# A streaming encoder step: where the attention's reciprocal and the split of a head pair's outputs stand in their turns

## The chip, the cores and the metric

The kernel runs as one program on one core of a Trainium2 chip. The metric is the device time of one execution in microseconds (us). The kernel before has been timed three times: 2195.16, 2206.37 and 2203.8 us, with a median of 2203.8 us. A further execution, which was profiled, took 2202.2 us, and all rows below come from that one.

## The reference, cut to what matters

One trunk layer of a chunk-causal encoder handles 1024 prompt frames and 64 sample frames (1088 columns in all, model width 1024, 16 heads of 64). The part that matters here is the attention beside the input projection:

```
h = rms_norm(x, norm_mix)
glu_a, glu_b, q, k, v, gates = split(h @ w_in)
u = glu_a * sigmoid(glu_b);  c = causal_dwconv(u, width 31);  c = silu(layer_norm(c)) @ w_conv_out
sc = q @ k.T * dh**-0.5 + rel_bias          # each 64-frame chunk sees itself and the 8 chunks before
pr = softmax(sc, axis=-1)
a  = (pr @ v) @ w_att_out
x  = x + (sigmoid(gates_c) * c + sigmoid(gates_a) * a) @ w_out
```

A gated feed-forward block, an input embedding and a last norm follow. All of it is float32. The products with weights are made of three products each, since every float32 operand is split into a rounded high part and a remainder.

## The kernel before, in words

Activations lie feature by row, time by column. The first stage works through a list of units, each a 1024 x 128 slice of `w_in` of one kind: `gb` and `ga` (the two halves of the gated unit), `s` (branch gates), and `q`, `k`, `v` for one pair of heads. A unit is computed in three column groups (384, 384 and 320 columns). `mm3` makes the 24 matmuls of a group, and calls a hook once in the middle of them. `job_group` makes the group, lets the helper engines read its result out of PSUM (`evac`), and calls the same hook once more. So there are six calls a unit, one for every 12 projection matmuls. Between two units `w_ahead` splits the next weights (`w_split`, L134 on ScalarE and L135 on VectorE).

The hook is `tick`, and one call of it is a *turn*. Attention is threaded through the projections by it. A step of attention is one head and one block of 128 queries (the ninth block is the 64 sample queries). Each head pair has 18 steps, and each is carried over several turns:

- `step_S`: TensorE makes the scores into `s_ps`, and VectorE adds the bias and takes the row extreme in one instruction (L487), which also frees `s_ps`. The pool that holds `s_ps` has one buffer.
- `step_E`, at the end of the same turn: ScalarE takes the exponential and the row sums (L495).
- `step_R`, one turn later: VectorE takes the reciprocal of the sums (L517) and ScalarE scales the row by it (L518).
- `step_T`, two turns after the scores: TensorE transposes the probabilities into `t_ps` (L504) and ScalarE copies them to `pt` (L507). `t_ps` has one buffer as well.
- `step_PV`, in every second turn, once both heads of a pair have their `pt`: TensorE multiplies by the values into `o_ps` (L529, 20 matmuls at full length). `o_ps` also has one buffer.
- `step_AT`, before the change at the end of the turn after `step_PV`: `split_into` copies `o_ps` to the high part of `aT` on ScalarE (L170), subtracts on VectorE to get the remainder (L171), and GpSimd's queue stores `aT` (L537). L171 is the last reader of `o_ps`.

Each engine runs its instructions in the order in which the program issues them, and that order is written out by hand (`manual_schedule`): it is the order of the calls inside `tick` and of the code around it. Inside a turn `bg_tick` also issues pieces of the depthwise convolution (taps, L327, on VectorE) and, once all eight features are convolved, of the layer norm (on both helper engines). How many it issues follows from a budget counted in estimated TensorE time, not from what the engines do. A turn with `step_PV` is called an A turn below, the one after it a B turn. A turns come at the end of a column group, B turns in the middle of one.

Of the kernel before, what the change touches and what calls it, by code (L numbers as in the profile page):

```python
# [75 lines left out]
def encoder_step(ctx: ExitStack, tc: tile.TileContext, I, O):  # L76
    nc = tc.nc
# [90 lines left out]
    def split_into(dst, c0, n, src, scale=1.0):  # L168

        nc.scalar.activation(out=dst[:, 0, c0:c0 + n], in_=src, func=AF.Copy, scale=scale)  # L170
        nc.vector.scalar_tensor_tensor(out=dst[:, 1, c0:c0 + n], in0=src, scalar=scale,  # L171
                                       in1=dst[:, 0, c0:c0 + n].bitcast(F32), op0=ALU.mult, op1=ALU.subtract)
# [47 lines left out]
    with tc.manual_schedule():  # L220
# [53 lines left out]
        at = att.enter_context(tc.tile_pool(name="att", bufs=1))  # L274
# [29 lines left out]
        bg = []  # L304
        debt = [0.0]

        def bg_tick(budget, most):
            debt[0] = min(debt[0] + budget, 2.5)
            while bg and debt[0] > 0 and most > 0:
                cost, fn = bg.pop(0)  # L310
                fn()
                debt[0] -= cost
                most -= 1
# [144 lines left out]
        for h in range(2):  # L458
            nc.gpsimd.memset(ql[h][64 - 64 * h:128 - 64 * h, :].bitcast(F32), 0.0)
        pipe = []  # L460
        stages = {"e": [], "t": [], "pv": [], "at": []}

        def step_S(st):
            i, p, h = st["i"], st["p"], st["h"]
            c = cur[i]
            smp = p == 8
            m = SMP if smp else P
            q0 = P * p
            if smp:
                n, k0, b0 = PAST + SMP, SEQ, 0  # L470
            else:
                k0 = max(0, P * p - PAST)
                n = P * p + P - k0
                b0 = 640 - n
            st.update(m=m, n=n, vb=(8 if smp else k0 // P), q0=q0)
            nh, w = (2, n // 2) if n > 512 else (1, n)
            ps = ps_s.tile([P, 2, 512], F32, tag="s", name="s_ps")
            wm = max(w, 256)
            for x in range(nh):
                a = k0 + x * w  # L480
                nc.tensor.matmul(ps[0:m, x, 0:wm], lhsT=c["Q"][h][:, q0:q0 + m], rhs=c["K"][h][:, a:a + wm],
                                 start=True, stop=False)
                nc.tensor.matmul(ps[0:m, x, 0:wm], lhsT=ql[h][:, q0:q0 + m], rhs=c["K"][h][:, a:a + wm],  # L483
                                 start=False, stop=True)
            s = at.tile([P, 640], F32, tag="s", name="s", bufs=3)
            sm = at.tile([P, 3], F32, tag="sm", name="sm", bufs=6)
            nc.vector.tensor_tensor_reduce(  # L487
                out=s[0:m, 0:n].rearrange("p (x c) -> p x c", x=nh), in0=ps[0:m, 0:nh, 0:w],
                in1=c["bias"][h][0:m, b0:b0 + n].rearrange("p (x c) -> p x c", x=nh),
                scale=1.0, scalar=3e38, op0=ALU.add, op1=ALU.min, accum_out=sm[0:m, 0:1])  # L490
            st.update(s=s, sm=sm)

        def step_E(st):
            m, n, s, sm = st["m"], st["n"], st["s"], st["sm"]
            nc.scalar.activation(out=s[0:m, 0:n], in_=s[0:m, 0:n], func=AF.Exp, scale=-1.0, bias=sm[0:m, 0:1],  # L495
                                 accum_out=sm[0:m, 1:2])

        def step_T(st):
            m, n, s = st["m"], st["n"], st["s"]
            nb = (n + P - 1) // P  # L500
            ps = ps_t.tile([P, 1024], F32, tag="t", name="t_ps")
            for b in range(nb):
                w = min(P, n - b * P)
                nc.tensor.transpose(ps[0:w, b * P:b * P + m], s[0:m, b * P:b * P + w], ident[0:m, 0:m])  # L504
            pt = at.tile([P, 640], F32, tag="pt", name="pt", bufs=2)
            if m == P:
                nc.scalar.activation(out=pt[:, 0:n], in_=ps[:, 0:n], func=AF.Copy)  # L507
            else:
                nc.scalar.activation(out=pt[:, 0:512].rearrange("p (b q) -> p b q", q=P)[:, :, 0:m],
                                     in_=ps[:, 0:512].rearrange("p (b q) -> p b q", q=P)[:, :, 0:m], func=AF.Copy)  # L510
                nc.scalar.activation(out=pt[0:64, 512:512 + m], in_=ps[0:64, 512:512 + m], func=AF.Copy)
            st.update(pt=pt, nb=nb)

        def step_R(st):

            m, n, s, sm = st["m"], st["n"], st["s"], st["sm"]
            nc.vector.reciprocal(out=sm[0:m, 2:3], in_=sm[0:m, 1:2])  # L517
            nc.scalar.activation(out=s[0:m, 0:n], in_=s[0:m, 0:n], func=AF.Copy, scale=sm[0:m, 2:3])  # L518

        def step_PV(pair):  # L520

            st = pair[0]
            c, m, n, nb = cur[st["i"]], st["m"], st["n"], st["nb"]
            o_ps = ps_o.tile([P, 512], F32, tag="o", name="o_ps")
            for b in range(nb):
                w = min(P, n - b * P)
                for x in pair:
                    a = 64 * x["h"]
                    nc.tensor.matmul(o_ps[a:a + 64, 0:m], lhsT=c["v"][0:w, st["vb"] + b, a:a + 64],  # L529
                                     rhs=x["pt"][0:w, b * P:b * P + m], start=(b == 0), stop=(b == nb - 1))  # L530
            st["o"] = o_ps

        def step_AT(st):
            m = st["m"]
            aT = at.tile([P, 2, P], F32R, tag="aT", name="aT")
            split_into(aT, 0, m, st["o"][:, 0:m])
            dma_st(out=a_d[st["i"]][:, :, st["q0"]:st["q0"] + m], in_=aT[:, :, 0:m].bitcast(F32))  # L537

        pe_bg = []

        def tick(base=1.95):


            spent = base
            pair = len(stages["pv"]) == 2
            late = len(stages["t"]) > 1 or (stages["t"] and not pipe)
            if pair:
                spent += 0.218 * stages["pv"][0]["nb"] + 0.2
            if late:
                spent += 0.107 * ((stages["t"][0]["n"] + P - 1) // P)  # L550
            if pipe:
                spent += 0.5
            ready_at = bool(stages["at"])
            new = pipe.pop(0) if pipe else None
            if new is not None:
                step_S(new)
            for x in stages["e"]:
                step_R(x)
            stages["e"].clear()
            bg_tick(RATIO * spent, 1)  # L560
            if pair:
                step_PV(stages["pv"])
                stages["at"].append(stages["pv"][0])
                stages["pv"].clear()
            if late:
                st = stages["t"].pop(0)
                step_T(st)
                stages["pv"].append(st)
            if new is not None:
                step_E(new)  # L570
                stages["e"].append(new)
                stages["t"].append(new)
            if ready_at:
                step_AT(stages["at"].pop(0))
            if pe_bg:
                if pe_bg[0][0] <= 0:
                    pe_bg.pop(0)[1]()
                else:
                    pe_bg[0][0] -= 1
            bg_tick(0.0, 9)  # L580
# [55 lines left out]
        def job(kind, i):  # L636
            hl = job_begin(kind, i)
            for g in range(3):
                job_group(kind, i, g, hl)
                if g == 0:  # L640
                    w_ahead(1)

        def job_group(kind, i, g, hl):
            c0, n = GR[g]
            ps_full = pjp.tile([P, 512], F32, tag="pj", name="pj")
            mm3(ps_full[:, 0:n], hl, hT, c0, n, hook=tick)
            evac(kind, i, g, ps_full[:, 0:n])
            tick()
# [236 lines left out]
        xt = None  # L885
        for kind, i in order_1a[2:-1]:
            job(kind, i)
        while pipe or stages["t"] or stages["pv"] or stages["at"] or pe_bg or bg:
            tick()
        att.close()  # L890

# [67 lines left out]
        for f in range(KT):  # L959
# [14 lines left out]
            x = xc.tile([P, T], F32, tag="xc", name="x")  # L974
# [691 lines left out]
```

## Time and profile before

| | |
|---|---|
| median of three runs | 2203.8 us |
| profiled execution, its own time | 2202.2 us |
| its span, first to last instruction | 2200.0 us |
| busy share of the span | PE 95%, PEld 93%, DVE 62%, ACT 40%, POOL 10% |
| mean granted TensorE clock | 0.985 of full speed |
| stage with attention | from about 100 us to about 1005 us |

PE is TensorE's matmuls, PEld its weight loads, DVE is VectorE, ACT ScalarE, POOL GpSimd. A row of the trace names a line of the program, an engine, an operation, what it writes and from what. In brackets stands how long the engine sat idle ahead of it and which instruction ended that wait. The granted clock is told as a share of full speed: 1.00 is 2.4 GHz and 0.50 is 1.2 GHz. In a list of waits a line gives who waited, on whom, the total in us, how many times, and the longest.

### The profile page before, as it was taken

What the parts mean: (1) busy time and instruction counts of PE and PEld (TensorE: products, weight loads), DVE (VectorE), ACT (ScalarE), POOL (GpSimd) and SP (SyncE); (2) the same over time, 40 slices, a digit from 0 to 9 for tenths busy, and PEclk for the clock granted to TensorE, in tenths of its full rate; (3) what the DMA queues carried; (4) which work ended last, traced back from release to release, by engine and by line L of the source; (5) the groups of instructions that cost most, each with busy time, mean ns of one, the idle gap of its engine ahead of it and who ended that gap; (6) DMA issues with size and microseconds to landing.
All of it is one profiled execution on the core that took longest, in us unless ns stands there. A gap on an engine that the chain in (4) does not pass through costs nothing.

```text
span 2200.0 us, 35326 instructions
## 1 busy us (share of the span) xinstructions
PE 2100.2 (95%) x14472; PEld 2039.9 (93%) x14472; DVE 1359.4 (62%) x2310; ACT 872.3 (40%) x1695; POOL 230.7 (10%) x455
## 2 busy tenths in 40 slices
PE   8989999999999998979999999999999999999997
PEld 6979898888888898879999999999999999999997
DVE  6777777777777663444235467777777763345644
ACT  5453635455555445574012334333333332112421
POOL 5100101101010101111000000000000020000400
PEclk9999999999999999999999999999999999999999
DMA  3312121212121221113433331212212144331011
GB/s 137 104 35 90 64 77 57 92 49 89 50 86 50 92 73 58 69 49 140 185 135 130 116 130 59 89 62 86 89 59 89 70 159 168 123 121 45 10 58 54
DMA packets 64706, 192.53 MB, mean 88 GB/s; under 512 B 8368, under 2 KB 22976, under 8 KB 63200
## 3 DMA queue, kind: packets, MB, share of 16 engines
q1 hardware_dynamic: 43072, 104.00, 13.9%
q0 software_dynamic: 21328, 85.71, 10.9%
q8 instruction: 114, 1.87, 0.3%
q10 hardware_dynamic: 144, 0.56, 0.1%
q14 instruction: 48, 0.39, 0.1%
HBM read 146.18 MB, written 54.01 MB: 91 GB/s over the span
## 4 chain that ended last, share of the span: by engine, by line
PE 50%; DVE 3%; issue 3%; ACT 2%; DMA 0%; POOL 0%; POOLq 0%; DVEq 0%; ACTq 0%
PE pj L1175 7%; PE pj L1176 7%; PE pj L1174 7%; PE pj L159 7%; PE pj L160 6%; PE pj L161 6%; PE pj L1477 3%; PE pj L1476 3%; PE pj L1475 3%; DVE acc L1021 1%; PE o_ps L529 0%; ACT tmp L1020 0%; ACT s L495 0%; ACT c L407 0%; PE t_ps L504 0%
## 5 line engine op out<-in xcount | busy, mean ns | idle before, releaser
L159 PE MATMUL pj<-hT,whl 128*128 128x384 f32 (+1 forms) x1296 | 445.6, 344 | 5.6 <-ACT kst L708 2.4
L161 PE MATMUL pj<-hT,whl 128*128 128x384 f32 (+1 forms) x1296 | 427.9, 330 | 0.3 <-DVE whl L135 0.3
L160 PE MATMUL pj<-hT,whl 128*128 128x384 f32 (+1 forms) x1296 | 427.7, 330 | 0.0
L327 DVE SCALAR_TENSOR_TENSOR c<-u,cc,c 128x1118 f32<-128x1118 f32 x240 | 329.7, 1374 | 3.4
L159 PEld LDWEIGHTS pj<-hT,whl 128*128 128x128 f32 x1296 | 247.4, 191 | 11.4 <-ACT kst L708 4.0
L160 PEld LDWEIGHTS pj<-hT,whl 128*128 128x128 f32 x1296 | 247.5, 191 | 0.0
L161 PEld LDWEIGHTS pj<-hT,whl 128*128 128x128 f32 x1296 | 246.7, 190 | 0.6 <-DVE whl L135 0.6
L1174 PE MATMUL pj<-mp,wq 128*128 128x272 f32 x704 | 203.9, 290 | 3.8 <-ACT ug L1250 2.7
L1176 PE MATMUL pj<-mp,wq 128*128 128x272 f32 x704 | 204.2, 290 | 0.0
L1175 PE MATMUL pj<-mp,wq 128*128 128x272 f32 x704 | 204.0, 290 | 0.0
L134 ACT ACTIVATE whl<-raw 128x1024 fp32r<-128x1024 f32 (+3 forms) x100 | 100.1, 1001 | 221.9 <-PE pj L1477 134.2
L518 ACT ACTIVATE s<-s,sm 128x640 f32<-128x640 f32 (+3 forms) x144 | 101.7, 706 | 194.2 <-DVE sm L517 192.7
L135 DVE TENSOR_TENSOR whl<-raw,whl 128x1024 fp32r<-128x1024 f32 (+3 forms) x100 | 115.7, 1158 | 91.9 <-ACT whl L134 91.8
L487 DVE CUSTOM_DVE_ANT_0 s<-s_ps,bias 128x640 f32<-128x640 f32 (+3 forms) x144 | 95.6, 664 | 110.9 <-PE s_ps L483 94.1
L1151 ACT ACTIVATE wq<-raw 128x512 fp32r<-128x512 f32 x144 | 84.3, 625 | 189.9 <-DVE raw L1160 135.6
L1476 PE MATMUL pj<-gp,whl 128*128 128x384 f32 (+1 forms) x432 | 141.2, 327 | 0.3 <-DVE gp L1385 0.3
L1477 PE MATMUL pj<-gp,whl 128*128 128x384 f32 (+1 forms) x432 | 141.2, 327 | 0.2 <-DVE whl L135 0.2
L1475 PE MATMUL pj<-gp,whl 128*128 128x384 f32 (+1 forms) x432 | 140.9, 326 | 0.0
L1175 PE MATMUL pj<-bq,wq 128*128 128x272 f32 x480 | 138.6, 289 | 0.0
L1176 PE MATMUL pj<-bq,wq 128*128 128x272 f32 x480 | 138.3, 288 | 0.0
L1174 PE MATMUL pj<-bq,wq 128*128 128x272 f32 x480 | 138.2, 288 | 0.0
L1174 PEld LDWEIGHTS pj<-mp,wq 128*128 128x128 f32 x704 | 133.8, 190 | 4.3 <-ACT ug L1250 2.9
(258 smaller groups left out, 4844.5 us busy)
## 6 DMA issues: line engine op xcount, KB each, us to landing
raw<-in_w_in SPq DMA_DIRECT2D x56, 512.0 KB, 3.2
raw<-in_w_ffn_up SPq DMA_DIRECT2D x44, 512.0 KB, 4.2
q_d<-ug POOLq DMA_DIRECT2D x22, 544.0 KB, 3.0
gp<-q_d POOLq DMA_DIRECT2D x22, 544.0 KB, 7.1
tg<-s_d POOLq DMA_DIRECT2D x16, 544.0 KB, 3.9
aP<-a_d POOLq DMA_DIRECT2D x8, 1088.0 KB, 6.0
a_d<-aT POOLq DMA_DIRECT2D x64, 128.0 KB, 2.2
f_d<-e_d POOLq DMA_DIRECT2D x16, 383.5 KB, 5.0
```

What stands on the lines that cost most here:

```text
L135: nc.vector.tensor_tensor(out=hl[:, 1, 0:k, :], in0=raw[:, 0:k, :], in1=hl[:, 0, 0:k, :].bitcast(F32), op=ALU.subtract)
L159: nc.tensor.matmul(ps, lhsT=wsel(hl, 0, k), rhs=r[:, 0, c0:c0 + n], start=(k == 0), stop=False)
L160: nc.tensor.matmul(ps, lhsT=wsel(hl, 0, k), rhs=r[:, 1, c0:c0 + n], start=False, stop=False)
L161: nc.tensor.matmul(ps, lhsT=wsel(hl, 1, k), rhs=r[:, 0, c0:c0 + n], start=False, stop=(k == K - 1))
L327: nc.vector.scalar_tensor_tensor(out=c_t[f], in0=u_t[f][:, j:j + CCOL], scalar=pc("conv_dw", f * CW + j), in1=c_t[f], op0=ALU.mult, op1=AL ...
L518: nc.scalar.activation(out=s[0:m, 0:n], in_=s[0:m, 0:n], func=AF.Copy, scale=sm[0:m, 2:3])
L1174: nc.tensor.matmul(ps, lhsT=q[:, 0, kt, :], rhs=h, start=start and kt == 0, stop=False)
L1175: nc.tensor.matmul(ps, lhsT=q[:, 0, kt, :], rhs=l, start=False, stop=False)
L1176: nc.tensor.matmul(ps, lhsT=q[:, 1, kt, :], rhs=h, start=False, stop=stop and kt == 3)
L1475: nc.tensor.matmul(ps, lhsT=hl[:, 0, k, :], rhs=h, start=k == 0, stop=False)
L1476: nc.tensor.matmul(ps, lhsT=hl[:, 0, k, :], rhs=l, start=False, stop=False)
L1477: nc.tensor.matmul(ps, lhsT=hl[:, 1, k, :], rhs=h, start=False, stop=k == K - 1)
```

## The change

VectorE's reciprocals of the waiting steps move out of `step_R` to the head of the turn, ahead of `step_S`. The line that scales the row stays where it was. `step_AT` moves from the end of the next turn to the place right behind `step_PV`, so the list of pairs that waited for it goes.

```diff
-        stages = {"e": [], "t": [], "pv": [], "at": []}
+        stages = {"e": [], "t": [], "pv": []}
...
         def step_R(st):
 
             m, n, s, sm = st["m"], st["n"], st["s"], st["sm"]
-            nc.vector.reciprocal(out=sm[0:m, 2:3], in_=sm[0:m, 1:2])
             nc.scalar.activation(out=s[0:m, 0:n], in_=s[0:m, 0:n], func=AF.Copy, scale=sm[0:m, 2:3])
...
-            ready_at = bool(stages["at"])
+            for x in stages["e"]:
+                nc.vector.reciprocal(out=x["sm"][0:x["m"], 2:3], in_=x["sm"][0:x["m"], 1:2])
             new = pipe.pop(0) if pipe else None
             if new is not None:
                 step_S(new)
...
             bg_tick(RATIO * spent, 1)
             if pair:
                 step_PV(stages["pv"])
-                stages["at"].append(stages["pv"][0])
+                step_AT(stages["pv"][0])
                 stages["pv"].clear()
             if late:
                 st = stages["t"].pop(0)
                 step_T(st)
...
-            if ready_at:
-                step_AT(stages["at"].pop(0))
...
-        while pipe or stages["t"] or stages["pv"] or stages["at"] or pe_bg or bg:
+        while pipe or stages["t"] or stages["pv"] or pe_bg or bg:
```

Two lines fewer in front of it move the line numbers behind the change: L517 for the reciprocal becomes L553, L518 for the scaling becomes L517; the evacuation of `u`, L666 before, is L664 after.

The places shown are an A turn of the third head pair and the B turn behind it, with a weight split between them. In the trace of before this is the stretch from 381.4 to 392.1 us. First VectorE's queue before; L487 is the read of the scores (its second row the row extreme), L327 a tap, L135 the remainder of the split weights:

```order
L487 ISA s,sm<-s_ps,bias 128x640
L487 ISA sm 128x1
L517 RECIPROCAL sm<-sm 128x1
L327 SCALAR_TENSOR_TENSOR c<-u,cc,c 128x1118 x2
L135 TENSOR_TENSOR whl<-raw,whl 128x1024
L487 ISA s,sm<-s_ps,bias 128x640
L487 ISA sm 128x1
L517 RECIPROCAL sm<-sm 128x1
L327 SCALAR_TENSOR_TENSOR c<-u,cc,c 128x1118
L171 SCALAR_TENSOR_TENSOR aT<-o_ps,aT 128x128
```

And VectorE's queue in the same two turns after the change:

```order
L553 RECIPROCAL sm<-sm 128x1
L487 ISA s,sm<-s_ps,bias 128x640
L487 ISA sm 128x1
L327 SCALAR_TENSOR_TENSOR c<-u,cc,c 128x1118
L171 SCALAR_TENSOR_TENSOR aT<-o_ps,aT 128x128
L327 SCALAR_TENSOR_TENSOR c<-u,cc,c 128x1118
L135 TENSOR_TENSOR whl<-raw,whl 128x1024
L553 RECIPROCAL sm<-sm 128x1
L487 ISA s,sm<-s_ps,bias 128x640
L487 ISA sm 128x1
L327 SCALAR_TENSOR_TENSOR c<-u,cc,c 128x1118
```

The reciprocal now stands ahead of the read of the new scores, and the remainder L171 stands in the A turn, between two taps, where it stood at the end of the B turn.

ScalarE's queue in the same two turns, before; L518 scales, L507 copies `pt`, L495 is the exponential, L134 the high part of the weights, L170 the high part of the outputs:

```order
L518 ACTIVATE s<-s,sm 128x640
L507 ACTIVATE pt<-t_ps 128x640
L495 ACTIVATE s,sm<-s,sm 128x640
L134 ACTIVATE whl<-raw 128x1024
L518 ACTIVATE s<-s,sm 128x640
L507 ACTIVATE pt<-t_ps 128x640
L495 ACTIVATE s,sm<-s,sm 128x640
L170 ACTIVATE aT<-o_ps 128x128
```

And after, where L517 is the scaling:

```order
L517 ACTIVATE s<-s,sm 128x640
L170 ACTIVATE aT<-o_ps 128x128
L507 ACTIVATE pt<-t_ps 128x640
L495 ACTIVATE s,sm<-s,sm 128x640
L134 ACTIVATE whl<-raw 128x1024
L517 ACTIVATE s<-s,sm 128x640
L507 ACTIVATE pt<-t_ps 128x640
L495 ACTIVATE s,sm<-s,sm 128x640
```

The copy L170 moved from the end of the B turn to the second place of the A turn, ahead of the copy of `pt` and the exponential. Which instructions there are, and TensorE's order, stay as they were.

## Rows read from the trace of the kernel before

**Rows 1.** The list of waits of TensorE over the whole span: who waited, for whom, us in total, times, longest.

```profile
PE o_ps L529 <- DVE aT L171: 51.8, 49, 3.4
PE o_ps L529 <- DVE sm L517: 6.3, 5, 1.3
PE s_ps L481 <- DVE sm L487: 2.7, 3, 1.6
```

**Rows 2.** Busy time by stretch: the stage with attention, and one pair of turns from the start of the scores of one A turn to the next. Columns: the stretch and its length, then busy us and instructions of PE, PEld, DVE, ACT and POOL, the granted clock, the DMA share and GB/s.

```profile
60.00:1012.00 952.00, 877.96 (x6050) 831.45 (x6049) 626.80 (x999) 497.84 (x1079) 106.64 (x204) 0.98 0.21 70
381.36:389.80 8.44, 7.94 (x63) 7.46 (x63) 6.88 (x12) 4.57 (x9) 0.67 (x1) 1.00 0.10 26
```

**Rows 3.** Groups of instructions by line over the whole span: busy us, mean ns of one, then the engine's idle time just ahead of them and what ended it.

```profile
L518 ACT ACTIVATE s<-s,sm 128x640 f32<-128x640 f32 (+3 forms) x144 | 101.7, 706 | 194.2 <-DVE sm L517 192.7 <-DVE lacc L348 0.7
L495 ACT ACTIVATE s<-s,sm 128x640 f32<-128x640 f32 (+3 forms) x144 | 99.9, 694 | 2.2 <-DVE sm L487 2.2
L487 DVE CUSTOM_DVE_ANT_0 s<-s_ps,bias 128x640 f32<-128x640 f32 (+3 forms) x144 | 95.6, 664 | 110.9 <-PE s_ps L483 94.1 <-issue 13.8 <-POOL u L660 2.9
L507 ACT ACTIVATE pt<-t_ps 128x640 f32<-128x640 f32 (+4 forms) x128 | 71.1, 556 | 8.7 <-PE t_ps L504 8.3
L517 DVE RECIPROCAL sm<-sm 128x1 f32<-128x1 f32 x144 | 22.5, 156 | 0.0
L327 DVE SCALAR_TENSOR_TENSOR c<-u,cc,c 128x1118 f32<-128x1118 f32 x240 | 329.7, 1374 | 3.4
L171 DVE SCALAR_TENSOR_TENSOR aT<-o_ps,aT 128x128 fp32r<-128x128 f32 (+1 forms) x72 | 20.4, 284 | 96.5 <-ACT aT L170 96.4
```

**Rows 4.** Instructions in order of time through the A and B turn whose queues are shown above, up to the products of the next A turn. Columns: start, duration, engine, line, operation, and in brackets the idle time ahead of it and what ended it.

```profile
381.36 0.31 PE L481 MATMUL s_ps<-K,Q 128*128 128x320 f32 x1
...
381.81 0.31 PE L483 MATMUL s_ps<-K,QL 128*128 128x320 f32 x1
...
382.62 1.31 PE L529 MATMUL o_ps<-pt,v 128*64 128x128 f32 x20 [0.50 <-DVE aT L171]
...
383.86 0.76 PE L504 MATMUL t_ps<-ident,s 128*128 128x128 f32 x5
...
386.08 1.05 ACT L134 ACTIVATE whl<-raw 128x1024 fp32r<-128x1024 f32 x1
...
386.56 0.31 PE L481 MATMUL s_ps<-K,Q 128*128 128x320 f32 x1
...
387.14 0.71 PE L504 MATMUL t_ps<-ident,s 128*128 128x128 f32 x5
...
387.16 1.23 DVE L135 TENSOR_TENSOR whl<-raw,whl 128x1024 fp32r<-128x1024 f32 x1 [0.62 <-ACT whl L134]
...
388.30 0.82 DVE L487 CUSTOM_DVE_ANT_0 s<-s_ps,bias 128x640 f32<-128x640 f32 x1
...
389.30 0.83 ACT L518 ACTIVATE s<-s,sm 128x640 f32<-128x640 f32 x1 [2.17 <-DVE sm L517]
...
389.80 0.29 PE L481 MATMUL s_ps<-K,Q 128*64 128x288 f32 x1
...
390.03 0.69 ACT L507 ACTIVATE pt<-t_ps 128x640 f32<-128x640 f32 x1
...
390.20 0.29 PE L483 MATMUL s_ps<-K,QL 128*64 128x288 f32 x1
...
390.62 0.82 ACT L495 ACTIVATE s<-s,sm 128x640 f32<-128x640 f32 x1
...
391.43 0.26 ACT L170 ACTIVATE aT<-o_ps 128x128 fp32r<-128x128 f32 x1
...
391.72 0.29 DVE L171 SCALAR_TENSOR_TENSOR aT<-o_ps,aT 128x128 fp32r<-128x128 f32 x1 [1.24 <-ACT aT L170]
...
392.07 1.31 PE L529 MATMUL o_ps<-pt,v 128*64 128x128 f32 x20 [1.58 <-DVE aT L171]
```

**Rows 5.** Instructions in order of time at an A turn whose products did not wait: the last score matmul and the first products.

```profile
815.97 0.31 PE L483 MATMUL s_ps<-K,QL 128*128 128x320 f32 x1
...
816.21 0.55 PE L529 MATMUL o_ps<-pt,v 128*64 128x128 f32 x6
```

**Rows 6.** Busy time by stretch, columns as in rows 2: the five stretches of the attention in which the granted clock lies under 1.00.

```profile
100.00:170.00 70.00, 61.69 (x449) 56.46 (x449) 47.27 (x82) 37.27 (x84) 6.24 (x11) 0.93 0.12 38
573.00:633.00 60.00, 53.53 (x404) 49.59 (x404) 41.35 (x73) 34.55 (x76) 7.60 (x15) 0.97 0.18 59
682.00:742.00 60.00, 53.50 (x405) 49.54 (x404) 41.34 (x73) 34.58 (x76) 6.98 (x11) 0.97 0.14 44
803.00:880.00 77.00, 69.18 (x506) 64.41 (x505) 30.23 (x65) 45.47 (x91) 10.44 (x20) 0.93 0.18 61
922.00:1008.00 86.00, 71.95 (x505) 65.96 (x504) 38.65 (x75) 58.53 (x105) 11.20 (x19) 0.92 0.17 56
```

**Rows 7.** Instructions in order of time: the products of two A turns in the stretch with the layer norm.

```profile
853.78 2.40 PE L529 MATMUL o_ps<-pt,v 128*64 128x128 f32 x20 [3.15 <-DVE aT L171]
...
961.83 1.31 PE L529 MATMUL o_ps<-pt,v 128*64 128x128 f32 x20 [1.88 <-DVE aT L171]
```

**Rows 8.** Busy time by stretch, columns as in rows 2: the two stretches where layer norm and attention run together.

```profile
840.00:870.00 30.00, 24.06 (x168) 22.13 (x167) 13.92 (x25) 19.24 (x34) 4.28 (x10) 0.84 0.24 80
950.00:1000.00 50.00, 40.71 (x286) 37.19 (x287) 23.00 (x42) 36.44 (x60) 6.17 (x10) 0.87 0.13 43
```

## The prediction

> **What bounds the kernel now.** I read the busy shares first: TensorE is busy nearly all the time, the helpers are not. So the question is what TensorE waits for, and the list of its waits gives one dominant answer [rows 1]. The products with the values, L529, wait 51.8 us for L171, the remainder of the outputs of the pair before, and 6.3 us more in five cases that are put down to the reciprocal: 58.1 us in 54 waits. In the stage with attention TensorE is busy 878.0 of 952 us [rows 2], so this is most of its 74 us of idle time. Nothing else in that list that the change touches is above 3 us.
>
> Then the instructions in order of time [rows 4]. The products at 392.07 wait 1.58 us for the single buffer `o_ps`. Followed back: L171 at 391.72, the copy at 391.43, the exponential at 390.62, the copy of `pt` at 390.03, the scaling at 389.30. The scaling waited 2.17 us for the reciprocal, which stood behind the read of the scores at 388.30, and that behind the split of the weights at 387.16. The output being split had been complete at 382.62 + 1.31 = 383.93, eight microseconds before its last reader ran. It was late by its place in two queues only. In the groups ScalarE idles 192.7 us in 144 scalings for the reciprocal (1.34 us a turn), and VectorE 96.4 us ahead of L171 for the copy [rows 3].
>
> **The products' wait.** After the change L171 is issued one turn earlier. I replay the pair from the durations of the trace, with 0 at the first score matmul of the A turn (381.36). A product that did not wait began 0.24 us after the start of the last score matmul [rows 5]; here that is at 0.45 + 0.24 = 0.69, and it ends at 2.00. Transposes follow 1.24 us after the start of the products (382.62 to 383.86), the next scores 2.70 us after those (to 386.56), the B transposes 0.58 later, and the next A scores 2.66 after them (387.14 to 389.80): 1.93, 4.63, 5.21, 7.87 [rows 4]. So a pair takes 7.87 us instead of 8.44.
>
> Now the helpers, in the new order, in this pair, which has the weight split and so is the tightest. The scaling runs from 0 to 0.75, since its reciprocal no longer waits for the scores. ScalarE copies the outputs at 2.05 to 2.3. The transposes end at 2.7, `pt` is copied to 3.35, the exponential ends at 4.15, the high part of the weights (1.05) at 5.2. VectorE reads the scores from 0.85 to 1.7, makes a tap (1.37) to 3.1, the remainder L171 (0.29) to 3.4, another tap to 4.75, waits, and splits the weights (1.23) to 6.45. Reciprocal to 6.6, read of the B scores to 7.45. ScalarE: scaling to 7.4, `pt` to 8.05, exponential to 8.8. TensorE's next scores at 7.87 need that read (7.45), and the next products at 0.69 + 7.87 = 8.56 need that `pt` (8.05). Both are there with 0.4 to 0.5 us to spare; `o_ps` has been free since 3.4. The two edits need each other here: with L171 moved alone, `pt` of before (390.03 + 0.69 = 390.72) would come 0.3 us after the products could begin (390.20 + 0.24). In a pair without a weight split the reads come over a microsecond earlier. So in the stretches with convolution alone the wait goes: gain 58.1 us. An idle time in the trace counts from the modelled end of the matmul ahead, and the products in [rows 5] began 0.07 us before that end (816.28), so another 54 x 0.07 = 3.8 us goes with it.
>
> **What the clock gives back.** In five stretches the granted clock is under full speed [rows 6]; the time lost to it is 70 x 0.07 + 60 x 0.03 + 60 x 0.03 + 77 x 0.07 + 86 x 0.08 = 20.8 us. The drops follow long waits of the products: the 20 matmuls at 853.78 took 2.40 us after a wait of 3.15 us, twice the ordinary 1.31, though a wait of 1.88 us at 961.83 was followed by none [rows 7]. With the waits gone I take all 20.8 us back, and count below what does not come.
>
> **What is kept.** While layer norm runs beside attention, ScalarE also squares, scales or takes tanh in each turn. In 950 to 1000 us it is busy 36.44 us. TensorE is busy 40.71 us there, and 50 x 0.13 = 6.5 us of these are lost to the clock, so it would need only 34.2 us; in 840 to 870 us it is 19.24 us against 24.06 - 30 x 0.16 = 19.3 [rows 8]. Without its waits TensorE would outrun ScalarE. How densely ScalarE can be filled no row shows; I assume nine tenths, so these stretches shrink to 36.44 / 0.9 = 40.5 and 19.24 / 0.9 = 21.4 us, and 6.3 + 2.1 = 8.4 us of the gain are kept. For new short waits in the tight turns I allow 1 us in each of the eight head pairs: 8 us. This last is bounded by 0 (the replay's spare time) and by the same turns' present waits, some 1.58 us in two weight-split turns a head pair, 25 us. I take a third because the replay shows spare time, though little.
>
> **What costs nothing.** No instruction is added or dropped. VectorE now waits inside the A turn for the copy of the outputs: from 1.7 to 2.35 at worst, when no tap stands between, which its free time covers (6.88 us busy of 8.44 [rows 2], 87% of 7.87). If that cover went, the read of the next scores would come late and TensorE would wait for `s_ps`, at 2.7 us in all today [rows 1]. GpSimd's stores follow L171, one a pair as before.
>
> The sum, on the profiled execution's own time: 2202.2 - 58.1 - 3.8 - 20.8 + 8.4 + 8 = 2135.9, say **2136 us**, 3.0% under it. The median of the three runs is 2203.8, 1.6 us above that execution, well inside their spread of 11 us, so I leave it.
>
> **Rivals.**
> *Everything goes* (13%). ScalarE fills its queue without gaps and no turn waits: 2202.2 - 82.7 = 2120 us. For it: the spare time in the replay. Against: the two stretches in [rows 8].
>
> *Half goes* (15%). The tight turns keep their waits, now for `pt` or the scores' reads: 25 us in the weight-split turns and about 10 of the 18 or so around the layer norm. Then 58.1 - 35 = 23 us go with the seam's 3.8, and the clock still falls, since it is the long waits that it follows: 2202.2 - 27 = 2175 us. For it: the split of the weights holds both helpers just where the new reciprocal stands behind it. Against: 0.4 us to spare there.
>
> *No change* (5%). The stage would be bound by something that the change leaves alone, the taps on VectorE say; then the waits move elsewhere, and it ends near 2201 us. Against: VectorE is busy 626.8 of 952 us [rows 2].
>
> *Slower* (7%). VectorE reads new scores only after the reciprocal, which needs the exponential of the turn before. If ScalarE runs late, so does that read, and TensorE's next scores wait for `s_ps`. In [rows 4] the exponential at 390.62 ends at 391.44, and its row sums some 0.1 later, about 1.0 us after the scores (390.49). If one turn in each of the 72 pairs passed that on, 74 us would be added and only 62 removed, with the clock as it is: 2214 us. It decides from 0.86 us a pair. Against: this exponential was late because its scaling waited for the reciprocal, and that is what goes.
>
> The Trainium skill speaks for this rival: its page "TensorE: Matmul & The Clock Gate" (Architectural detail) says that the queues of ScalarE and VectorE are strictly first in, first out. By that rule alone a copy that must wait for the products holds back the `pt` and the exponential behind it, and the remainder holds back the next reciprocal. The trace agrees that nothing overtakes: VectorE idled those 96.4 us ahead of L171 with taps queued behind it [rows 3]. By the rule the new stall of VectorE is up to 0.65 us in each of 72 pairs, some 47 us in place of the 96.4 that it loses there now, and it reaches TensorE only where VectorE has no time to spare.
>
> **How the numbers follow.** The forecast (60%) has its own range, 2124 to 2156: the lower end has ScalarE full and a third of the allowance, the upper end the full 25 us (17 more) and some 3 us of the clock still lost. With the rivals the range is 2114 to 2178; outside it lie the slower case, no change, and a few per cent beyond 2114. Faster by over 0.5%, which is about what a measurement of this kernel can tell from no change, has 0.88; within it 0.05; slower 0.07.
>
> **What would show it.** Right: the products' wait for L171 is gone from TensorE's list, or under 5 us; ScalarE's idle time ahead of the scaling falls from 193 us to less than half; the granted clock is 1.00 in most of the stretches in [rows 6]; the last attention products end some 60 to 70 us earlier. Wrong: TensorE waits more than 20 us for the reads of the scores or for `pt`, or the clock still falls in five stretches although the waits are gone. If VectorE's idle time ahead of L171 grows over 96 us and the read of the scores is what TensorE waits for, it was the slower case.

## The result, and the profile after

The changed kernel took 2126.6 us (median of four runs, 2123.92 to 2127.75) against 2200.2 us for the kernel before on the same chip: a ratio of 0.9662, with a 95% interval of 0.9632 to 0.9693. The forecast was 2136 us, and faster; the time lies 9 us under it, in the forecast's own range of 2124 to 2156 us. The execution profiled after took 2126.3 us, 75.9 us less than the one before.

Two lines of the list of TensorE's waits over the whole span after the change, those of the scores and of the products. The columns are total us, times, longest; L528 is the products with the values, L529 before:

```profile
PE s_ps L481 <- DVE sm L487: 2.0, 3, 1.0
PE o_ps L528 <- ACT pt L507: 2.0, 4, 0.9
```

These two lines answer to [rows 1]. The wait for L171, 58.1 us in 54 cases, is gone. Of the products' waits 2.0 us are left, and they are now for the copy of `pt`.

Busy time by stretch after, columns as in [rows 2]. The first stretch ends, like the first of [rows 2], 0.85 us after the start of the matmul that opens the last unit of the projection, and the second is the rest:

```profile
60.00:934.00 874.00, 859.06 (x6053) 817.01 (x6052) 630.00 (x1000) 505.86 (x1080) 104.63 (x205) 1.00 0.23 76
934.00:2124.50 1190.50, 1170.70 (x8157) 1167.15 (x8155) 694.83 (x1238) 343.78 (x555) 93.26 (x215) 0.99 0.28 99
```

The stage shrank from 952 to 874 us, by 78.0. TensorE's idle time in it went from 952 - 878.0 = 74.0 to 874 - 859.1 = 14.9 us, so 59.1 us of the gain are idle time. The other 18.9 us are busy time: the same matmuls took less of it, and the granted clock of the stage reads 1.00 where it was 0.98. The rest of the program, where no attention runs, took 1190.5 us, 2.5 us more than before; in a second trace of the changed kernel it was 1189.1 us, so part of this is scatter.

The groups after, with the columns of [rows 3]:

```profile
L517 ACT ACTIVATE s<-s,sm 128x640 f32<-128x640 f32 (+3 forms) x144 | 101.2, 703 | 66.9 <-DVE sm L553 66.6
L495 ACT ACTIVATE s<-s,sm 128x640 f32<-128x640 f32 (+3 forms) x144 | 100.7, 699 | 7.4 <-DVE sm L487 7.4
L487 DVE CUSTOM_DVE_ANT_0 s<-s_ps,bias 128x640 f32<-128x640 f32 (+3 forms) x144 | 95.2, 661 | 77.1 <-PE s_ps L483 64.9 <-issue 9.5 <-POOL u L658 2.6
```

And three lines of VectorE's list of waits:

```profile
DVE s L487 <- PE s_ps L483: 64.9, 72, 2.4
DVE sm L553 <- ACT s L495: 31.5, 39, 1.9
DVE aT L171 <- ACT aT L170: 21.9, 19, 3.3
```

The instructions take as long as before. ScalarE's idle time ahead of the scaling fell from 192.7 to 66.6 us, VectorE's ahead of L171 from 96.4 to 21.9. New is VectorE's wait for the exponential ahead of the reciprocal, 31.5 us in all; ahead of the reciprocal of before it idled 0.0 us [rows 3].

The pair of turns of [rows 4] after the change, in order of time:

```profile
358.32 0.31 PE L481 MATMUL s_ps<-K,Q 128*128 128x320 f32 x1
...
358.77 0.31 PE L483 MATMUL s_ps<-K,QL 128*128 128x320 f32 x1
...
359.01 1.31 PE L528 MATMUL o_ps<-pt,v 128*64 128x128 f32 x20
...
360.25 0.77 PE L504 MATMUL t_ps<-ident,s 128*128 128x128 f32 x5
...
360.37 0.28 ACT L170 ACTIVATE aT<-o_ps 128x128 fp32r<-128x128 f32 x1 [0.35 <-PE o_ps L528]
...
361.16 0.28 DVE L171 SCALAR_TENSOR_TENSOR aT<-o_ps,aT 128x128 fp32r<-128x128 f32 x1
...
363.55 1.22 DVE L135 TENSOR_TENSOR whl<-raw,whl 128x1024 fp32r<-128x1024 f32 x1 [0.81 <-ACT whl L134]
...
364.76 0.80 DVE L487 CUSTOM_DVE_ANT_0 s<-s_ps,bias 128x640 f32<-128x640 f32 x1
...
365.68 0.68 ACT L507 ACTIVATE pt<-t_ps 128x640 f32<-128x640 f32 x1
...
366.20 0.29 PE L481 MATMUL s_ps<-K,Q 128*64 128x288 f32 x1
...
366.82 1.31 PE L528 MATMUL o_ps<-pt,v 128*64 128x128 f32 x20
```

From the first scores to the next A scores it is 366.20 - 358.32 = 7.88 us, where it was 8.44 and the replay had 7.87. The products follow the last score matmul by 0.24 us. L171 ends at 361.44, 3.1 us into the pair (replay 3.4), the read of the B scores at 7.2 (7.45), the copy of `pt` at 8.04 (8.05).

### The profile page after: what moved, and what is told of

The parts are those of the page before. It is cut to its first block, busy times and chain, and to the rows that moved or that the text cites. A ratio compares the mean times of both kernels' runs of the same rounds, so it can differ in the third digit from the quotient of the medians.

```text
span 2124.5 us, 35326 instructions
## 1 busy us (share of the span) xinstructions
PE 2081.9 (98%) x14472; PEld 2026.0 (95%) x14472; DVE 1362.2 (64%) x2310; ACT 880.3 (41%) x1695; POOL 228.1 (11%) x455
## 4 chain that ended last, share of the span: by engine, by line
PE 53%; DVE 3%; ACT 3%; issue 2%; DMA 0%; POOL 0%; POOLq 0%; DVEq 0%; ACTq 0%
PE pj L1173 7%; PE pj L1174 7%; PE pj L1172 7%; PE pj L159 7%; PE pj L161 7%; PE pj L160 7%; PE pj L1474 3%; PE pj L1475 3%; PE pj L1473 3%; DVE acc L1019 1%; ACT tmp L1018 0%; DVE tmp L187 0%; ACT s L517 0%; PE sp_ps L216 0%; ACT c L407 0%
## 5 line engine op out<-in xcount | busy, mean ns | idle before, releaser
L327 DVE SCALAR_TENSOR_TENSOR c<-u,cc,c 128x1118 f32<-128x1118 f32 x240 | 330.9, 1379 | 2.8
L159 PEld LDWEIGHTS pj<-hT,whl 128*128 128x128 f32 x1296 | 244.1, 188 | 11.0 <-ACT kst L706 4.0
L161 PEld LDWEIGHTS pj<-hT,whl 128*128 128x128 f32 x1296 | 244.0, 188 | 0.6 <-DVE whl L135 0.6
L160 PEld LDWEIGHTS pj<-hT,whl 128*128 128x128 f32 x1296 | 244.4, 189 | 0.0
L134 ACT ACTIVATE whl<-raw 128x1024 fp32r<-128x1024 f32 (+3 forms) x100 | 100.3, 1003 | 222.8 <-PE pj L1475 135.2
L135 DVE TENSOR_TENSOR whl<-raw,whl 128x1024 fp32r<-128x1024 f32 (+3 forms) x100 | 115.7, 1158 | 77.4 <-ACT whl L134 77.0
L487 DVE CUSTOM_DVE_ANT_0 s<-s_ps,bias 128x640 f32<-128x640 f32 (+3 forms) x144 | 95.2, 661 | 77.1 <-PE s_ps L483 64.9
L1172 PEld LDWEIGHTS pj<-mp,wq 128*128 128x128 f32 x704 | 133.9, 190 | 5.4 <-ACT ug L1248 2.9
L1173 PEld LDWEIGHTS pj<-mp,wq 128*128 128x128 f32 x704 | 133.9, 190 | 0.0
```

The costliest lines, as they stand in the source:

```text
L134: nc.scalar.activation(out=hl[:, 0, 0:k, :], in_=raw[:, 0:k, :], func=AF.Copy)
L135: nc.vector.tensor_tensor(out=hl[:, 1, 0:k, :], in0=raw[:, 0:k, :], in1=hl[:, 0, 0:k, :].bitcast(F32), op=ALU.subtract)
L159: nc.tensor.matmul(ps, lhsT=wsel(hl, 0, k), rhs=r[:, 0, c0:c0 + n], start=(k == 0), stop=False)
L160: nc.tensor.matmul(ps, lhsT=wsel(hl, 0, k), rhs=r[:, 1, c0:c0 + n], start=False, stop=False)
L161: nc.tensor.matmul(ps, lhsT=wsel(hl, 1, k), rhs=r[:, 0, c0:c0 + n], start=False, stop=(k == K - 1))
L327: nc.vector.scalar_tensor_tensor(out=c_t[f], in0=u_t[f][:, j:j + CCOL], scalar=pc("conv_dw", f * CW + j), in1=c_t[f], op0=ALU.mult, op1=AL ...
```

## The experiments

All were timed beside the kernel before on the same chip. The changed kernel was timed again beside the split behind `pt`, the split ahead of the first tap and the second pass of ScalarE. The other four ran on another chip, where the kernel before took 2199.0 us against 2200.3 us, so that they are held against the changed kernel across two chips.

**The changed kernel again**, as the measure for the others.

> The changed kernel once more, on the chip of the next three, so that they can be held against it: 2122 to 2130 us by every theory.

2127.4 us, ratio 0.9672 (0.9648 to 0.9695).

**The reciprocal alone.** The kernel before, with the reciprocal moved to the head of the turn:

```diff
@@ tick, kernel before
             ready_at = bool(stages["at"])
+            for x in stages["e"]:
+                nc.vector.reciprocal(out=x["sm"][0:x["m"], 2:3], in_=x["sm"][0:x["m"], 1:2])
@@ step_R
-            nc.vector.reciprocal(out=sm[0:m, 2:3], in_=sm[0:m, 1:2])
```

> The kernel before with one half of the change: the reciprocal leads the turn, the outputs are still split at the end of the B turn. Theory A (both places cost, each part of the 58 us): in pairs without a weight split the exponential of the B turn ends about 7.6 us into the pair and the remainder L171 at 8.1, ahead of the next products at 8.6, so no wait; with a weight split L171 ends at 9.4 and the products wait 0.85 us, in about 16 pairs, 13 us; beside the layer norm they wait some 2 us in half of the pairs, 9 us, and the clock still falls there, 6 us. So about 2127 + 28 = 2155 us, with some 20 to 25 us of waits of L529 for L171. Theory B (the place of the split alone is the cause): 2195 to 2205 us and over 45 us of waits. Theory C (the late scaling alone is the cause): 2125 to 2132 us.

2148.2 us, ratio 0.9762 (0.9740 to 0.9784). From TensorE's list of waits:

```profile
PE o_ps L528 <- DVE aT L171: 19.0, 21, 2.5
...
PE o_ps L528 <- DVE sm L554: 1.4, 5, 0.3
```

20.4 us of the 58.1 are left, as theory A had it: 11.6 us in the first six head pairs, where it had 13, and 8.9 us in the last two, where it had 9. The time is 7 us under its 2155; B and C are out. An earlier scaling makes `pt`, the exponential and so the copy of the outputs earlier, even where the copy keeps its late place.

**The split alone.** The changed kernel, with the reciprocal back behind the read of the scores:

```diff
@@ tick, changed kernel
-            for x in stages["e"]:
-                nc.vector.reciprocal(out=x["sm"][0:x["m"], 2:3], in_=x["sm"][0:x["m"], 1:2])
@@ step_R
+            nc.vector.reciprocal(out=sm[0:m, 2:3], in_=sm[0:m, 1:2])
```

> The kernel before with the other half: the outputs are split in the turn of their products, the reciprocal stands behind the read of the scores as before. Theory A: the wait for L171 is gone; in the weight-split turns the copy of pt comes at 8.95 us into the pair and the products at 8.56 wait 0.4 us, about 6 us in all; beside the layer norm they wait 0.6 us, with a weight split 2.6 us, about 12 us, and the clock falls once or twice, 3 us. So about 2127 + 21 = 2148 us, TensorE's waits being for the copy L507 of pt. Theory B: 2125 to 2130 us. Theory C: 2185 us or more.

2144.6 us, ratio 0.9743 (0.9724 to 0.9763), again near theory A's 2148. Its lines of TensorE's waits:

```profile
PE o_ps L529 <- ACT pt L507: 6.7, 7, 1.7
PE s_ps L481 <- DVE sm L487: 3.4, 3, 2.0
```

With `o_ps` free in time, what the products wait for is `pt`, which needs the scaling, which needs the reciprocal. But these waits are 6.7 us where theory A had 18, and nearly all lie beside the layer norm. Much of the rest stands in no line of the list. Held against the changed kernel matmul by matmul, this run loses 7.4 us up to 700 us, some 0.4 us in each of 18 turns. The products that took 1.31 us at 366.82 in the changed kernel are these here:

```profile
370.09 0.69 ACT L507 ACTIVATE pt<-t_ps 128x640 f32<-128x640 f32 x1
...
370.48 1.65 PE L529 MATMUL o_ps<-pt,v 128*64 128x128 f32 x20
```

The 20 matmuls alternate between two heads. They begin while the second head's `pt` is still being copied, until 370.78, and take 1.65 us. A late `pt` shows here as a longer group, inside TensorE's busy time, and not as a wait. That is theory A's 0.4 us in the weight-split turns.

So each half alone is worth 51 to 54 us against 2199.0 us for the kernel before in that call, and both together 73: they share most of the gain, and neither brings the rest.

**The split behind the exponential.** The changed kernel, but `step_AT` at the end of its A turn:

```diff
@@ tick, changed kernel
             if pair:
                 step_PV(stages["pv"])
-                step_AT(stages["pv"][0])
+                done = stages["pv"][0]
                 stages["pv"].clear()
...
                 stages["t"].append(new)
+            if pair:
+                step_AT(done)
```

> The changed kernel, but the outputs are copied and split at the end of the A turn, behind the exponential, not right behind the products. If strict order on ScalarE and VectorE costs something (the copy that waits for the products holds back pt and the exponential, the remainder holds back the taps), this is faster than the changed kernel: up to 0.2 us in each of 72 pairs, 2112 us. Theory A: the copy stands in time that ScalarE spends waiting for the transposes, and L171 has 4 us to spare at either place: 2123 to 2131 us, and no waits of L529 for L171 over 1 us in all.

2135.4 us (2133.46 to 2138.92), ratio 0.9704 (0.9683 to 0.9725): outside what either theory gave, and slower than the changed kernel by 8 to 9 us, whose eight runs all lie between 2123.9 and 2130.6. (The intervals of the two ratios, 0.9683 to 0.9725 here and 0.9648 to 0.9695 there, overlap a little; the runs do not.) So the copy does not hold back anything that matters where it stands in the change; standing behind the exponential is what costs. From the list of waits, VectorE's and then TensorE's:

```profile
DVE aT L171 <- ACT aT L170: 76.2, 60, 3.6
```

```profile
PE s_ps L481 <- DVE sm L487: 4.6, 4, 1.5
PE o_ps L528 <- ACT pt L507: 4.5, 5, 1.9
```

VectorE waits 76.2 us for the copy instead of 21.9, and the reads of the scores and `pt` come late in a few turns. One of them, in order of time:

```profile
895.26 0.29 DVE L171 SCALAR_TENSOR_TENSOR aT<-o_ps,aT 128x128 fp32r<-128x128 f32 x1 [3.01 <-ACT aT L170]
895.47 1.31 DVE L419 SCALAR_TENSOR_TENSOR c<-lacc,c 128x1118 f32<-128x1118 f32 x1
896.70 0.15 DVE L553 RECIPROCAL sm<-sm 128x1 f32<-128x1 f32 x1
896.77 0.80 DVE L487 CUSTOM_DVE_ANT_0 s<-s_ps,bias 128x640 f32<-128x640 f32 x1
...
897.64 0.41 PE L481 MATMUL s_ps<-K,Q 128*128 128x320 f32 x1 [0.69 <-DVE sm L487]
```

The read of the scores stands behind L171's stall of 3.01 us with VectorE busy all the way (L419 is a piece of the layer norm), and TensorE waits for it; in the changed kernel these scores did not wait.

**The split behind `pt`**, to see whether that wait is the cause:

```diff
@@ tick, changed kernel
             if pair:
                 step_PV(stages["pv"])
-                step_AT(stages["pv"][0])
+                done = stages["pv"][0]
                 stages["pv"].clear()
...
                 stages["pv"].append(st)
+            if pair:
+                step_AT(done)
```

> The changed kernel, but the outputs are copied and split behind the copy of pt and ahead of the exponential: between the changed kernel and the one with the split behind the exponential, which came out at 2135 us where I had 2123 to 2131. Theory D (VectorE's wait ahead of L171 holds back the taps and layer-norm pieces behind it, and it is the place of the copy on ScalarE that sets this wait: 22 us in the changed kernel, 76 us behind the exponential): the copy comes 1.2 us later than in the changed kernel and 0.9 us earlier than behind the exponential, so about half of the 9 us: 2129 to 2133 us, with VectorE's wait ahead of L171 at 35 to 60 us. If the loss came from the exponential's own place (a later copy can only help pt and the exponential), 2124 to 2128 us.

2128.8 us (2128.31 to 2129.79), ratio 0.9678 (0.9657 to 0.9699). VectorE's wait came out in the middle, as theory D had it:

```profile
DVE aT L171 <- ACT aT L170: 43.3, 38, 2.8
```

But the time is only 1.3 us over the changed kernel's in the same call, within what these runs scatter, so it does not tell the two theories apart.

**The split ahead of the first tap**, a stall of VectorE alone:

```diff
@@ tick, changed kernel
-            bg_tick(RATIO * spent, 1)
             if pair:
                 step_PV(stages["pv"])
                 step_AT(stages["pv"][0])
                 stages["pv"].clear()
+            bg_tick(RATIO * spent, 1)
```

> The changed kernel, but products and split are issued ahead of the first background piece of the turn, so VectorE meets L171 straight behind the read of the scores and waits for the copy, about 0.65 us in each of 72 pairs, 47 us where it waits 22 now. Theory A: in the convolution turns this stays within VectorE's free time, beside the layer norm it costs a little, also because ScalarE's layer-norm piece now stands behind the copy, ahead of pt: 2126 to 2136 us. If every stall of VectorE reached TensorE: 2127 + 25 to 47, about 2165 us.

2126.9 us, ratio 0.9669 (0.9647 to 0.9691): no difference. The wait that I had worked out as 47 us came:

```profile
DVE aT L171 <- ACT aT L170: 46.1, 69, 3.7
```

A stall of VectorE of that size, in 69 of 72 pairs, cost nothing that these runs can tell. Together the four places give 22, 43, 46 and 76 us of it for 2127, 2129, 2127 and 2135 us. That the loss at the last place is the stall passing VectorE's spare time fits these, and the trace of that run shows it in part: held against the changed kernel matmul by matmul, four losses that follow such a stall, straight or by way of a late reciprocal, at 145, 898, 899 and 927 us, come to 3.9 of the 10.4 us that it loses in the stage. For the rest, that it is the stall and nothing else about the later place was not shown.

**More work for ScalarE.** The changed kernel with a second pass over each scaled row, by one, in place; it adds work and leaves nothing out:

```diff
@@ step_R, changed kernel
             nc.scalar.activation(out=s[0:m, 0:n], in_=s[0:m, 0:n], func=AF.Copy, scale=sm[0:m, 2:3])
+            nc.scalar.activation(out=s[0:m, 0:n], in_=s[0:m, 0:n], func=AF.Copy)
```

> The changed kernel with a second pass of ScalarE over each scaled row, a copy in place, 0.6 us more in each of 144 turns, 86 us of ScalarE's time in all. It measures how much spare time the helpers have. Theory A (the replay: TensorE sets the pace, ScalarE is full only beside the layer norm, where it was busy 36.6 of 40 us): in the convolution turns nothing shows, in a weight-split turn pt comes 0.1 us late; beside the layer norm ScalarE has 1.2 us more in each of about 8 pairs and less than 0.8 to spare, so some 8 us, and 3 to 5 us of clock: about 2140 us. If ScalarE is as full all along as I allowed in the forecast (spare time of a third of a microsecond in the tight turns, waits in all head pairs), 16 weight-split pairs lose 0.7 us too: 2152 us. If nothing is spare, all of it passes: about 2210 us.

2146.1 us, ratio 0.9758 (0.9733 to 0.9783): 19 us for 74 us of added busy time, between theory A and the allowance. The first line of its profile page and of that of the changed kernel, one after the other:

```profile
PE 2089.1 (97%) x14472; PEld 2029.5 (95%) x14472; DVE 1365.1 (64%) x2310; ACT 954.7 (45%) x1839; POOL 228.1 (11%) x455
```

```profile
PE 2081.9 (98%) x14472; PEld 2026.0 (95%) x14472; DVE 1362.2 (64%) x2310; ACT 880.3 (41%) x1695; POOL 228.1 (11%) x455
```

Held against the changed kernel matmul by matmul, it falls behind in two ways. Up to the layer norm it loses some 8 us, mostly in steps of 0.3 to 0.4 us at a turn with a weight split, again inside the products' groups. So about 0.9 us of the 1.2 added to a pair is spare even there. Beside the layer norm it loses the other 11.

**The old order for the last two head pairs only:**

```diff
@@ step_R, kernel before
-            nc.vector.reciprocal(out=sm[0:m, 2:3], in_=sm[0:m, 1:2])
+            if st["i"] >= 6:
+                nc.vector.reciprocal(out=sm[0:m, 2:3], in_=sm[0:m, 1:2])
@@ tick
+            for x in stages["e"]:
+                if x["i"] < 6:
+                    nc.vector.reciprocal(out=x["sm"][0:x["m"], 2:3], in_=x["sm"][0:x["m"], 1:2])
...
-                stages["at"].append(stages["pv"][0])
+                if stages["pv"][0]["i"] >= 6:
+                    stages["at"].append(stages["pv"][0])
+                else:
+                    step_AT(stages["pv"][0])
```

> Both edits are undone for the last two head pairs (6 and 7), which run beside the layer norm, and kept for the first six. Waits of L529 before that fall to these two pairs were about 18 us, and half clock beside them cost time as well. If the falls of the clock follow the long waits, both come back in this stretch: 18 - 3 of waits and 8 to 12 of clock, 2127 + 25 = 2152 us, with the granted clock under 1.00 there and nowhere else in the attention. If the clock falls for another reason, it falls in the first six pairs too or not at all, and the time is near 2127 + 15 = 2142 us.

2148.6 us, ratio 0.9763 (0.9741 to 0.9786). Its products' wait, and its busy time by stretch up to and from 790 us; the last two head pairs begin at 749 us, their long waits at 801 us:

```profile
PE o_ps L530 <- DVE aT L171: 18.4, 12, 3.4
```

```profile
60.00:790.00 730.00, 720.45 (x5056) 686.63 (x5054) 553.16 (x865) 402.49 (x889) 82.42 (x165) 1.00 0.24 77
790.00:945.00 155.00, 132.27 (x910) 124.41 (x911) 69.45 (x131) 96.41 (x180) 18.43 (x32) 0.93 0.18 60
```

The waits come back in this stretch and the clock falls there, to 0.93, and nowhere before it in the attention. So the falls came back with the waits; the other reading is out. The two head pairs' share of the gain is 2148.6 - 2127 = about 22 us, of which 18.4 - 2.0 = 16.4 are the products' waits.

The products' waits are not all that goes with a fall. One is left in the changed kernel, behind a wait of 1.15 us, at 841.9 us, that the transposes of the values (L722) have for a layer-norm instruction on VectorE:

```profile
842.00:846.00 4.00, 4.00 (x16) 4.00 (x17) 0.00 (x0) 0.49 (x1) 1.75 (x1) 0.58 0.38 135
```

The kernel before waited 1.18 us there and had no fall behind it. What decides between the two no run here shows.

## Why the prediction was right, and where its sizes were off

*The products' wait.* Right in kind and size: 58.1 us went down to 2.0, and TensorE's idle time in the stage by 59.1. The replay of the tightest pair was met within 0.3 us at every point compared. That the two edits need each other holds where the replay said it, in the turns with a weight split: there the split alone loses some 0.4 us a turn, where the replay gave 0.3. For the kernel as a whole each edit alone brings most of the gain, and the pair together 18 to 22 us more than either.

*The clock.* The step is right: both the old order in two head pairs and the whole change show it. Its size of 20.8 us, the share of the granted clock times the length of the stretch, is an upper bound. The stage lost 18.9 us of busy time, in which the seam is contained; with the seam at 3.8 us by the forecast, or some 5.5 as estimated below, 13 to 15 us are the clock's, net of the one fall that is left. A granted clock that is low while TensorE waits costs nothing, and the stretches of [rows 6] hold such waits.

*What is kept.* This is the term that was mis-sized: 8.4 + 8 = 16.4 us were to be kept of the 82.7, and the stage kept 82.7 - 78.0 = 4.7. None of that lies in TensorE's idle time, which fell by 59.1 us; it lies in the busy time, where 18.9 us came of the 20.8 + 3.8.

Of the 8 us for new short waits in the eight head pairs only 0.4 came as listed waits in the six that run beside the convolution: spare time of 0.4 us in a replay is spare time, and the second pass of ScalarE found about 0.9 us of it.

For the 8.4 us, the two stretches of [rows 8] are these after, matmul for matmul, columns as there:

```profile
786.20:806.60 20.40, 20.21 (x168) 18.69 (x167) 14.14 (x25) 17.91 (x33) 4.00 (x8) 1.00 0.35 112
883.20:922.10 38.90, 36.39 (x287) 32.87 (x287) 22.49 (x42) 36.91 (x62) 6.18 (x10) 1.00 0.18 65
```

20.4 and 38.9 us, against 21.4 and 40.5: near, but partly by luck. ScalarE, nine tenths full, was to set these lengths. It is busy 88% and 95%, but TensorE is busy 20.2 of 20.4 and 36.4 of 38.9 us, so that its own work fills them. That need was set too low, at 19.3 and 34.2 us, since the clock's whole share had been taken off busy time, and its idle time too high, at 2.1 and 6.3 us; the two errors nearly cancel.

With 4.7 us in the place of 16.4, and the 2.5 us that the rest of the program took more, the sum would be 2136 - 11.7 + 2.5 = 2126.8 us.

*The signs.* ScalarE's idle time ahead of the scaling did fall to less than half, the granted clock is 1.00 in all five stretches of [rows 6], and the last attention products begin 78 us earlier, where 60 to 70 were forecast.

*The seam*, 3.8 us: the 0.24 us between scores and products is there in the pair shown. Its sum can be told apart from the clock's where the granted clock is 1.00 before and after. These are the same matmuls, before and then after, columns as in [rows 2]:

```profile
170.00:573.00 403.00, 380.07 (x2611) 361.98 (x2610) 294.96 (x448) 199.17 (x450) 44.71 (x87) 1.00 0.22 75
157.60:539.30 381.70, 377.92 (x2611) 361.49 (x2611) 295.76 (x448) 203.70 (x452) 42.37 (x87) 1.00 0.23 79
```

21 of the waits lay there, and the busy time fell by 2.1 us, 0.10 us a wait; over 54 that makes an estimate of some 5.5 us, rather more than 3.8.

*The rivals.* "Everything goes", 2120 us, was nearer than its 13% suggests: in the ten microseconds from 890 us ScalarE was busy without a break. "Half goes" is what either edit alone does in kind: part of the waits stays, and the clock still falls beside the layer norm. "Slower" put its finger on a real wait, VectorE's for the exponential, 31.5 us in all; but TensorE's wait for the reads of the scores did not grow, 2.0 us after 2.7. VectorE's stall ahead of L171, 0.65 us at worst in the replay, was up to 3.3 us long, though in 19 turns only and 21.9 us in all. The rule of the Trainium skill's page "TensorE: Matmul & The Clock Gate" (Architectural detail) that the queues of ScalarE and VectorE are strictly first in, first out agrees with the traces here: VectorE's stalls of 22 to 76 us ahead of L171 moved with the place of the copy. Their price in these runs was nothing clear of the scatter up to 46 us, and 8 to 9 us at 76.

## What to carry to other kernels

Where an engine waits for a single buffer, look at when the data in it was complete and at what its last reader stood behind in its own queue: here 8 us of place in two queues, not of work. Issue a small instruction that frees a buffer or feeds another engine ahead of the read that has to wait, and the reader of a result near its maker, but not behind work of the second engine that it does not need. A replay of one tight turn by durations from the trace tells what such a move leaves. Count lost clock on busy time alone, and look for a late operand in a group that takes longer too, not only in the list of waits.

## What was not expected

Either edit alone brought 51 to 54 us of the 73. A later place for the copy, which I had thought free, cost 8 to 9 us, while a stall of VectorE in 69 of 72 pairs cost nothing that these runs can tell. And the layer norm's longer stretch, where ScalarE is busy 95%, left TensorE only 2.5 of 38.9 us idle.
